# The first two key-cache loads of the sample tokens wait for the queries

## The chip, the core and the metric

The kernel runs on one core of a Trainium2 chip. The metric is the device time of one execution, in microseconds (us). A core has five engines that work side by side, each through its own queue in order: TensorE (PE; PEld is its loading of weights), VectorE (DVE), ScalarE (ACT), GpSimd (POOL) and SyncE (SP). Transfers between the chip's main memory and the on-chip memory are issued from the queues of SP, ACT and POOL and carried out by 16 DMA engines that all of them share. Matmul results go to PSUM, a small memory of eight banks.

## The reference, cut to what matters

The program is one step of one layer of a decoder, for a prompt of 512 tokens and eight sample tokens (one for each of eight sequences). One normalised input feeds a dilated sliding-window attention in three groups and an RWKV-7 time mixing; both are merged, projected, and followed by a SwiGLU network. For the sample tokens the attention reads keys and values from a cache:

```python
def dilated_window_sample(q, k_all, v_all, window, dilation, buf_len):
    T = q.shape[1]
    span = window // dilation
    idx = buf_len + jnp.arange(T)[:, None] - dilation * jnp.arange(span + 1)[None, :]
    ...
    kg = k_all[:, idx_c].astype(jnp.float32)
    vg = v_all[:, idx_c].astype(jnp.float32)
    s = jnp.einsum('bqhd,bqmhd->bhqm', q.astype(jnp.float32), kg) * HEAD_DIM ** -0.5
    p, lse = masked_softmax(s, valid[None, None])
    o = jnp.einsum('bhqm,bqmhd->bqhd', p, vg)
    return o, lse.transpose(0, 2, 1)
```

So each sample token has, for each group and head, one query, 128 cached keys and values, and its own key and value.

## The kernel before

All 520 tokens (512 + 8) go through the big products together, as two chunks of 260 columns. Each fp32 product is made of three matmuls of a shorter format: input and weights are both split in a high and a low part (`hh`/`hl` or `hu`/`lu` for the input, `whi`/`wlo` for the weights), and high x high, low x high and high x low are summed. A weight tile is loaded by SP into `raw` (512 KB), ScalarE writes `whi`, VectorE writes `wlo`.

At the start the input comes in eight tiles `xt` (260 KB each), six issued by SP and two by POOL (lines 667 to 671). Ahead of the normalisation the first products are made from the input times a weight vector only, `hu` and `lu` (lines 676 to 682), so that TensorE can begin before the sums of squares are there; `norm0` (line 703) then makes the normalised `hh` and `hl`, and half of the `hl` tiles are written by POOL (line 712).

What runs when is settled when the program is built, in two steps. A planner in the kernel (`Clocks` and `Weave`, lines 226 to 452) holds a guessed clock for each engine and a guessed cost for every instruction and transfer (a POOL load occupies POOL for 1.04 us and lands 2.7 us plus its size later). It takes the main sequence of products and the side jobs as generators, and lets that one go on whose next inputs are there by its clocks. What it writes down is then put in order once more for each engine, by a scheduler that takes what is ready; an instruction can so come to stand ahead of others that were written down before it. On the chip each queue runs in the order that came out, and an instruction whose inputs aren't there holds up all that stand behind it on its engine.

`sample_group(g)` (line 892) is such a side job, one for each of three groups. It waits until the eight query and key tiles of its group are there (line 900), lets TensorE transpose the sample columns `sga` and ScalarE copy them to `sv` (lines 903 to 910): `sv[:, 0]` are the queries, spread over 128 partitions. Then it goes through the cached keys in eight chunks of 256 KB. `cache` (line 915) loads a chunk into one of two buffers `kt` by POOL; VectorE multiplies it by the queries (line 925) and sums it into the scores `sc` (line 926). The chunk after it is always asked for one step ahead. After the softmax the values go the same way (lines 937 to 943, results in `so`), and the flag `sample` of the group is set, for which the next group's `sample_group` and the third group's first product wait. For the first group both buffers `kt` are new, so its first two loads depend on nothing that comes before them. All instructions are recorded with line 380, that of a wrapper, so the profile tells them apart by the names of their tiles.

Of the kernel before, what the change touches and what calls it, by code (L numbers as in the profile page):

```python
# [12 lines left out]
ALU = mybir.AluOpType  # L13
# [452 lines left out]
def program(tc, I, O):  # L466
    nc = tc.nc
    ck = Clocks()
    V, S, G, SY = (Unit(n, e, tc, ck) for n, e in (("DVE", nc.vector), ("ACT", nc.scalar), ("POOL", nc.gpsimd), ("SP", nc.sync)))
# [7 lines left out]
    def nm(s):  # L477
        uid[0] += 1
        return f"{s}_{uid[0]}"
# [196 lines left out]
    for k in range(KD):  # L676
        if k == 2:
            wsplit(first_w, first_raw, 4, 8)
        g = feat[:, F_MIX, k:k + 1]
# [212 lines left out]
    def sample_group(g):  # L892
# [14 lines left out]
        sv = sp.tile([128, 3, 64], FP, name=nm("sv"), tag="sv")  # L907
# [5 lines left out]
        KR = 8  # L913

        def cache(name, c):
            if c < 64:
                t = sp.tile([128, KR, 64], FP, name=nm("kt"), tag="kt", bufs=2)
                G.dma_start(out=t[:], in_=I[name][g, :, c:c + KR])
                return t
        yield from wv.take("kt")  # L920
        nxt = cache("kcache", 0)
        for c in range(0, 64, KR):
            kt, nxt = nxt, cache("kcache", c + KR)
            yield (kt,)
            V.tensor_tensor(out=kt[:], in0=kt[:], in1=_bc(sv[:, 0].unsqueeze(1), [128, KR, 64]), op=ALU.mult)
            V.tensor_reduce(out=sc[:, c:c + KR], in_=kt[:], op=ALU.add, axis=X)
            yield (sc,)
        t = sp.tile([128, 64], FP, name=nm("st"), tag="st")
# [6 lines left out]
        V.tensor_scalar(out=sc[:, 64:65], in0=sc[:, 64:65], scalar1=first[:], scalar2=None, op0=ALU.mult)  # L935
        V.tensor_reduce(out=so[:, g, 65:66], in_=sc[:], op=ALU.add, axis=X)
        nxt = cache("vcache", 0)
        for c in range(0, 64, KR):
            vt, nxt = nxt, cache("vcache", c + KR)
# [1194 lines left out]
```

## Time and profile before

| what | value |
|---|---|
| median of three runs | 1295.33 us (1294.89 to 1297.84) |
| the profiled execution's own time | 1299.81 us |
| its span | 1298.0 us |
| mean granted clock of TensorE | 0.985 |
| loads `kt<-kcache`, `kt<-vcache` | 24 each, 256 KB each |

The profile is of one execution. Its page gives the busy time of each engine and its share of the span, the DMA queues, and groups of instructions by tile; views of the trace give the instructions of one engine in order of time, who waited for whom, and tables by stretch. In a row such as "kt<-kcache" the tile that is written stands on the left and what is read on the right. In a timeline, the bracket behind a row is the idle time of that engine just ahead of it and what ended it. Busy times of TensorE are modelled ends of pipelined matmuls; the distance from start to start is the better measure of its pace.

### The profile page before, as it was taken

Reading aid. Unit: us, or ns where it says so; the run is one execution under the profiler, and the core shown is the slowest. Engines: PE = TensorE matmul, PEld = TensorE weight load, DVE = VectorE, ACT = ScalarE, POOL = GpSimd, SP = SyncE. Lnnn points to the kernel's source line nnn. Section 1 sums busy time; section 2 is a strip of 40 time slices with the busy share of each in tenths; the row PEclk is TensorE's granted clock in tenths of the full one; section 3 lists DMA queues with packets and bytes.
Section 4 is the critical chain, followed back from the end, with each engine's and each line's share of the span. In section 5 each row is a group of like instructions: output and inputs, shape, how many; then the busy total and the mean of one; then the engine's idle time right before and its main releaser. Section 6 shows DMA issues by size and latency. Waiting matters only on the chain.

```text
span 1298.0 us, 29596 instructions
## 1 busy us (share of the span) xinstructions
PE 1246.1 (96%) x11594; PEld 1178.2 (91%) x11594; DVE 933.4 (72%) x2448; ACT 648.2 (50%) x1638; POOL 176.0 (14%) x273
## 2 busy tenths in 40 slices
PE   7999999999989989999999999999999999999996
PEld 6998999989978888888888888999999999999996
DVE  6956866954769998879886765565798888873333
ACT  5244244266666655576775585323444444442220
POOL 1300100100123332122123112121000000010000
PEclk9999999999999999999998999999999999999998
DMA  6532654644245545553346355465233323343331
GB/s 218 157 95 91 209 178 146 208 137 160 73 121 152 145 143 149 153 156 104 89 126 184 101 168 169 139 218 191 92 99 98 98 98 98 98 143 90 90 103 66
DMA packets 93420, 173.76 MB, mean 134 GB/s; under 512 B 42672, under 2 KB 47824, under 8 KB 93280
## 3 DMA queue, kind: packets, MB, share of 16 engines
q1 hardware_dynamic: 60880, 102.46, 25.8%
q0 software_dynamic: 15792, 50.73, 12.9%
q10 hardware_dynamic: 16608, 18.68, 4.3%
q8 instruction: 91, 1.49, 0.5%
q14 instruction: 49, 0.40, 0.1%
HBM read 135.33 MB, written 30.07 MB: 127 GB/s over the span
## 4 chain that ended last, share of the span: by engine, by line
PE 59%; DVE 18%; issue 11%; DMA 6%; ACT 4%; POOL 2%; SPq 0%; ACTq 0%; DVEq 0%; POOLq 0%
PE mm L380 39%; PE ax L380 15%; PE ch L380 5%; DVE wlo L380 3%; DMA fb<-FD 1%; DVE X L380 1%; DVE xt L380 1%; DMA kt<-vcache 1%; DVE qk L380 1%; DVE raw L380 1%; DMA sw<-raw 1%; DVE sw L380 1%; DVE k L380 1%; DVE GH L380 1%; DVE oac L380 1%
## 5 line engine op out<-in xcount | busy, mean ns | idle before, releaser
L380 PE MATMUL mm<-hh,whi 128*128 128x260 f32 x1136 | 340.3, 300 | 0.8 <-ACT gt L380 0.8
L380 PE MATMUL mm<-hh,wlo 128*128 128x260 f32 x1136 | 326.0, 287 | 7.4 <-DVE wlo L380 7.0
L380 PE MATMUL mm<-hl,whi 128*128 128x260 f32 x1136 | 326.0, 287 | 0.0
L380 ACT CAST whi<-raw 128x1024 fp32r<-128x1024 f32 (+2 forms) x213 | 184.2, 866 | 255.8 <-PE mm L380 185.0
L380 DVE TENSOR_TENSOR wlo<-raw,whi 128x1024 fp32r<-128x1024 f32 (+2 forms) x213 | 211.5, 993 | 86.4 <-ACT whi L380 81.7
L380 PEld LDWEIGHTS mm<-hh,whi 128*128 128x128 f32 x1136 | 215.9, 190 | 13.3 <-issue 5.8
L380 PEld LDWEIGHTS mm<-hh,wlo 128*128 128x128 f32 x1136 | 216.0, 190 | 10.0 <-DVE wlo L380 9.2
L380 PEld LDWEIGHTS mm<-hl,whi 128*128 128x128 f32 x1136 | 215.9, 190 | 1.3
L380 PE MATMUL mm<-fh,whi 128*128 128x260 f32 x308 | 87.2, 283 | 0.3 <-DVE g L380 0.3
L380 PE MATMUL mm<-fh,wlo 128*128 128x260 f32 x308 | 87.1, 283 | 0.0
L380 PE MATMUL mm<-fl,whi 128*128 128x260 f32 x308 | 87.1, 283 | 0.0
L380 PE MATMUL mm<-h2l,whi 128*128 128x260 f32 x264 | 74.8, 283 | 0.0
L380 PE MATMUL mm<-h2h,wlo 128*128 128x260 f32 x264 | 74.6, 282 | 0.0
L380 PE MATMUL mm<-h2h,whi 128*128 128x260 f32 x264 | 74.6, 282 | 0.0
L380 PE MATMUL ax<-h2h,wlo 128*128 128x260 f32 x264 | 74.5, 282 | 0.0
L380 PE MATMUL ax<-h2l,whi 128*128 128x260 f32 x264 | 74.5, 282 | 0.0
L380 PE MATMUL ax<-h2h,whi 128*128 128x260 f32 x264 | 74.3, 281 | 0.0
L380 DVE TENSOR_TENSOR xt<-X,LT 128x60 f32<-128x60 f32 (+24 forms) x248 | 59.7, 241 | 3.6
L380 DVE TENSOR_TENSOR X<-X,xt 128x60 f32<-128x60 f32 (+24 forms) x248 | 56.1, 226 | 3.8
L380 PEld LDWEIGHTS mm<-fh,whi 128*128 128x128 f32 x308 | 58.1, 188 | 0.8 <-issue 0.4
L380 PEld LDWEIGHTS mm<-fh,wlo 128*128 128x128 f32 x308 | 57.9, 188 | 0.0
L380 PEld LDWEIGHTS mm<-fl,whi 128*128 128x128 f32 x308 | 57.9, 188 | 0.0
(427 smaller groups left out, 3122.0 us busy)
## 6 DMA issues: line engine op xcount, KB each, us to landing
raw<-w_in SPq DMA_DIRECT2D x77, 512.0 KB, 4.0
raw<-w_gate SPq DMA_DIRECT2D x22, 512.0 KB, 3.8
raw<-w_up SPq DMA_DIRECT2D x22, 512.0 KB, 3.8
raw<-w_down SPq DMA_DIRECT2D x16, 512.0 KB, 3.5
kt<-kcache POOLq DMA_DIRECT2D x24, 256.0 KB, 3.7
kt<-vcache POOLq DMA_DIRECT2D x24, 256.0 KB, 3.6
sw<-raw ACTq DMA_DIRECT2D x64, 65.0 KB, 3.7
GD<-gt ACTq DMA_DIRECT2D x16, 260.0 KB, 3.0
```

The source lines that it names most:

```text
L380: r = f(*a, **k)
```

## The change

In the first group (`g == 0`) and for the first two chunks of keys (`c < 2 * KR`, that is 0 and 8), POOL runs one small addition ahead of the load. It reads one column of the queries in `sv` and writes one column of the tile `kt`, which the load then fills over. As the load may only write the tile after that addition, and the addition needs `sv`, both loads come after the queries. What is computed stays the same, as the load replaces the column. The other 22 loads of keys and the 24 of values are as they were.

```diff
         def cache(name, c):
             if c < 64:
                 t = sp.tile([128, KR, 64], FP, name=nm("kt"), tag="kt", bufs=2)
+                if name == "kcache" and g == 0 and c < 2 * KR:
+
+                    G.tensor_tensor(out=t[:, 0, :1], in0=sv[:, 0, :1], in1=sv[:, 0, :1], op=ALU.add)
                 G.dma_start(out=t[:], in_=I[name][g, :, c:c + KR])
                 return t
```

`G` is POOL's wrapper, which also books the instruction on the planner's clock for POOL.

## The prediction

> **What bounds the kernel now.** I read the page first, then the waits of TensorE, and then the two stretches that the change touches: the first 20 us, where the two loads run now, and the time about 111 us, where the queries of the first group appear.
>
> ```profile
> span 1298.0 us, 29596 instructions
> ...
> PE 1246.1 (96%) x11594; PEld 1178.2 (91%) x11594; DVE 933.4 (72%) x2448; ACT 648.2 (50%) x1638; POOL 176.0 (14%) x273
> ```
>
> TensorE is busy for 1246.1 of 1298.0 us, so only 51.9 us can be won by anything that takes waits away, and a good part of these lies at the start. The next rows are the start in stretches of 1.5 us (columns: stretch, length, busy time and count on PE, PEld, DVE, ACT, POOL, then granted clock, busy share of the DMA engines, GB/s) and two rows of the DMA issues (size, and median us to landing).
>
> ```profile
> 3.00:4.50 1.50, 0.00 (x0) 0.00 (x0) 0.05 (x1) 0.00 (x0) 1.10 (x3) 1.00 0.99 316
> ...
> 9.00:10.50 1.50, 0.92 (x4) 0.62 (x4) 1.09 (x3) 0.73 (x1) 0.00 (x0) 1.00 1.01 370
> ...
> 16.50:18.00 1.50, 0.91 (x8) 0.69 (x6) 1.50 (x2) 1.50 (x5) 0.00 (x0) 1.00 1.01 385
> ```
>
> ```profile
> xt<-xT SPq DMA_DIRECT2D x6, 260.0 KB, 8.1
> kt<-kcache POOLq DMA_DIRECT2D x2, 256.0 KB, 7.0
> ```
>
> The DMA engines are full from 3 us to 18 us, and the two early key loads (512 KB) are in the middle of it: issued at 3.04 us and landed after 7.0, while the input tiles xt queue for 8.1 us. ScalarE waits for those tiles (timeline; in brackets the idle time before the row and its releaser):
>
> ```profile
> 8.21 0.61 ACT L380 CAST whi<-raw 128x512 fp32r<-128x512 f32 x1
> 9.35 0.73 ACT L380 ACTIVATE hu<-xt,feat 128x520 fp32r<-128x520 f32 x1 [0.53 <-DMA xt<-xT]
> 11.02 0.73 ACT L380 ACTIVATE hu<-xt,feat 128x520 fp32r<-128x520 f32 x1 [0.94 <-DMA xt<-xT]
> ```
>
> And TensorE waits behind it:
>
> ```profile
> 7.33 0.58 PE L380 MATMUL mm<-hu,whi 128*128 128x260 f32 x1 [7.33 <-ACT whi L380]
> ...
> 10.13 0.59 PE L380 MATMUL mm<-hu,whi 128*128 128x260 f32 x1 [0.58 <-ACT hu L380]
> ...
> 13.63 0.42 PE L380 MATMUL mm<-hu,whi 128*128 128x260 f32 x1
> 13.85 0.43 PE L380 MATMUL mm<-lu,whi 128*128 128x260 f32 x1
> 14.12 0.29 PE L380 MATMUL mm<-hu,wlo 128*128 128x260 f32 x1
> 14.24 0.28 PE L380 MATMUL mm<-hu,whi 128*128 128x260 f32 x1
> ...
> 18.04 0.39 PE L380 MATMUL mm<-hu,whi 128*128 128x260 f32 x1 [0.63 <-ACT raw L380]
> 39.27 0.39 PE L380 MATMUL mm<-hu,wlo 128*128 128x260 f32 x1 [0.82 <-DVE wlo L380]
> ```
>
> Its first matmul starts at 7.33 us, and from there to 110 us these are all the waits of its matmuls: 0.58, 0.63 and 0.82, together 2.03 us. That is what a better start can be worth, beside the matmuls' own pace.
>
> **The change: the start.** Taking 512 KB out of a full stretch that moves 316 to 370 GB/s frees 512/370 = 1.4 to 512/316 = 1.6 us of DMA time for the xt tiles behind it. ScalarE's two waits for xt, 0.53 and 0.94, make 1.47 us; I take both as gone (bounds 0 and 1.47: the tile of the 9.35 row would land about a microsecond sooner, and ScalarE is free for it at 8.21 + 0.61 = 8.82; the tile of the 11.02 row would land at about 9.5, when ScalarE has just ended the one before). TensorE's wait of 0.58 then shrinks by the same 0.53. The wait of 0.63 at 18.04 is the emptying of a PSUM bank that TensorE itself filled; it stays. The wait of 0.82 at 39.27 is for VectorE, whose work at the start hangs on ScalarE's and comes 1.47 sooner, while TensorE comes 0.53 sooner: VectorE gains 0.94 on it and the 0.82 go. Sum of the start: 0.53 + 0.82 = 1.35 us, with bounds of 0 and 2.03.
>
> **The change: about 111 us.** Now the other side (POOL first, then ScalarE's copies of the queries, VectorE's rows behind them, and TensorE's first use of the weights' low halves):
>
> ```profile
> 0.24 0.10 POOL L2126 MEMSET const-float32-0.0<- 128x1 f32 x1 [0.24 <-issue]
> ...
> 3.04 1.06 POOL L380 DMA_DIRECT2D kt<-kcache  x2
> 31.63 1.77 POOL L380 TENSOR_TENSOR hl<-hn,hh 128x520 fp32r<-128x520 f32 x1 [27.53 <-ACT hh L380]
> ...
> 54.49 3.62 POOL L380 TENSOR_TENSOR hl<-hn,hh 128x520 fp32r<-128x520 f32 x1 [3.44 <-ACT hh L380]
> ...
> 114.40 1.14 POOL L380 DMA_DIRECT2D kt<-kcache  x2 [41.93 <-DVE sc L380]
> ```
>
> ```profile
> 110.05 0.95 ACT L380 COPY sv<-ax 32x192 f32<-32x192 f32 x3
> ```
>
> ```profile
> 112.23 1.28 DVE L380 TENSOR_TENSOR kt<-kt,sv 128x512 f32<-128x512 f32 x2
> 113.43 1.27 DVE L380 TENSOR_REDUCE sc<-kt 128x8 f32<-128x512 f32 x2
> 114.76 1.22 DVE L380 TENSOR_TENSOR wlo<-raw,whi 128x1024 fp32r<-128x1024 f32 x1
> ```
>
> ```profile
> 118.20 0.29 PE L380 MATMUL mm<-hh,wlo 128*128 128x260 f32 x1
> ```
>
> The loads are written after the queries in the program, yet they head POOL's queue: its order is drawn up when the program is built, by what is ready. With the new instruction they are not ready before sv. Left at 3.04 us, they would hold up the hl rows at 31.63, on which the queries themselves depend, and the program could not end; so they go behind the last row before 114.40. Behind them in POOL's queue stands only the third load, which waits for VectorE's sc anyway: POOL sits idle 41.93 us there, and nobody else is delayed.
>
> sv is whole at 110.05 + 0.95 = 111.0. The new instruction writes one column of 128 partitions. No row shows it; its bounds are 0.10 (the memset of one column) and 3.62 (the slowest hl, 520 columns beside a busy VectorE). I take 0.3, nearest to the memset, with a little for two inputs. Then each load is issued and lands:
>
> ```profile
> L380 POOL DMA_DIRECT2D kt<-kcache x3: 536/541/543, 114.4 to 120.0; - x3
> ...
> DMA to landing us min/median/max: 3.3/3.5/4.9
> ```
>
> That row is of the next three loads of the same tile. The first lands at 111.0 + 0.3 + 3.5 = 114.8 (bounds 114.4 and 119.5), the second 0.3 + 0.54 later, at 115.6. Before, VectorE took them at 112.23: the samples' path is 2.6 us late. Its later links hang on each other, so it ends 2.6 us later too:
>
> ```profile
> 168.17 0.28 DVE L380 SCALAR_TENSOR_TENSOR so<-sv,sc,so 128x64 f32<-128x64 f32 x1
> ```
>
> ```profile
> L380 ACT COPY sv<-ax x4: 307/308/310, 205.1 to 209.2; 32x192 f32<-32x192 f32 x4
> ```
>
> The next group's queries come at 205.1, so the end may slip from 168.4 to 171.0 and nothing waits. What is displaced is VectorE's work, 1.28 + 1.27 = 2.55 us, and this has room in VectorE's idle time:
>
> ```profile
> 110.00:115.00 5.00, 5.00 (x47) 4.67 (x47) 4.25 (x8) 2.66 (x7) 0.54 (x2) 1.00 0.00 0
> ```
>
> ```profile
> 110.00:120.00 10.00, 10.00 (x86) 8.58 (x85) 8.47 (x24) 3.39 (x9) 1.08 (x2) 1.00 0.41 120
> 120.00:130.00 10.00, 10.00 (x81) 9.47 (x80) 8.11 (x21) 5.38 (x19) 1.61 (x3) 1.00 0.27 87
> 130.00:140.00 10.00, 10.00 (x97) 9.69 (x97) 7.57 (x14) 2.67 (x5) 1.07 (x2) 1.00 0.70 218
> ```
>
> VectorE is idle for 1.53 + 1.89 + 2.43 = 5.8 us from 110 to 140, twice what is displaced. The DMA engines stand still from 110 to 115 (share 0.00), so the two loads find them free. I cost this side at nothing, on the condition that VectorE's order, which is drawn up anew as well, puts the wlo row (114.76) ahead of the multiplications that now wait. If not, see the second rival.
>
> The Trainium skill speaks against this place: SBUF — State Buffer, "SBUF: two separate sides", says that a load issued from GpSimd can be starved while VectorE runs certain copies, because GpSimd cannot write its descriptors, and tells of about 3.1 us against 0.62. By it I estimate 2.5 us more on each of the two landings, 117.3 in place of 114.8. The rows of the next three loads, 536 to 543 ns to issue and 4.9 us to land at most beside a busy VectorE, show nothing of this size.
>
> **Sum.** 1.35 us off the profiled span, 1298.0 to 1296.65; with the 1.81 us around it (that execution took 1299.81) 1298.5. The runs shown have a median of 1295.33; the same step gives 1294.0.
>
> **The rivals.** *Hidden anyway:* the xt tiles land no sooner (the other loads take up the freed share), or TensorE's own pace at the start holds. For it: TensorE runs from 10.13 to 17 us almost without a wait. Against it: 0.58 and 0.82 have releasers behind the tiles. Time: 1295.3.
>
> *VectorE stands still (slower):* its queue keeps the multiplications where they are, at 112.23. VectorE then waits 114.8 - 112.2 = 2.6 us, and the second pair is done at about 117.5; wlo ends near 118.7, against its use at 118.20. It decides from the point where VectorE is over 118.20 - (114.76 + 1.22) = 2.2 us late. The price is 2.6 us there, and, as the samples' chunks stay 2.6 behind in a stretch where VectorE is busy for 9.35 of 10 us,
>
> ```profile
> 150.00:160.00 10.00, 10.00 (x87) 10.00 (x86) 9.35 (x17) 3.08 (x6) 2.09 (x4) 1.00 0.75 215
> ```
>
> a second 2.6 at most: 5.2 in all, less the 1.35 of the start: 1295.33 + 3.85 = 1299.2. Against it: until 140 us VectorE has those 5.8 us, and the order follows what is ready.
>
> *TensorE's pace steps up sooner:* matmuls start 0.22 us apart at 13.63 and 0.12 apart at 14.12 (the clock column says 1.00 throughout, so the pace is read from the starts). If the missing wait of 0.58 lets the step come as early as 10.13, some 17 matmuls (10.13 to 13.85 at 0.22) each save 0.10, 1.7 us; the low halves of the input come at VectorE's pace, so I count half, 0.85: 1293.1. The Trainium skill, TensorE: Matmul & The Clock Gate, "What's actually happening", has a window of some 3.4 us of steady work ahead of the full clock, and says that the window runs freely; by this the step would come either one whole window sooner or not at all.
>
> *A luckier order (faster):* everything after 111 us on VectorE is put in order again, and TensorE's waits for wlo change.
>
> ```profile
> PE mm L380 <- DVE wlo L380: 7.9, 7, 2.7
> ```
>
> Without the 0.82 at the start 7.1 us are left in six waits. If half of it goes, 3.5 us: 1290.5. No row says which way.
>
> **How the numbers follow.** Forecast 0.50; hidden 0.13; VectorE stands still 0.15; earlier step 0.08; luckier order 0.14. The range leaves about 0.1 out on each side: 1290.0 to 1299.5. A change of 0.3% is 3.9 us, about the least that a measurement of this kernel can tell from none: faster than 1291.4 is the luckier order and a tail of the others, 0.19; slower than 1299.2 about half of the standstill and unlucky orders, 0.13; the rest, 0.68, between. Forecast alone: 1293.3 to 1295.3.
>
> **What would show it.** Right: the kt loads issued after 111 us with a short POOL row each ahead of them; no wait of ScalarE for xt near 9 and 11 us; TensorE's waits near 10 and 39 us gone; wlo ahead of the first kt row in VectorE's queue. Wrong: xt landing as late as before; VectorE idle for over 2 us ahead of its first kt row, with TensorE waiting for wlo about 118 us; or waits of TensorE after 200 us that differ by more than the start gained.

## The result and the profile after

The changed kernel takes 1315.4 us (median of four runs, 1312.37 to 1328.0) against 1296.59 us for the kernel before, run beside it. The ratio is 1.0151, with a 95% interval from 1.0106 to 1.0196: slower by 1.5%, some 19 us, and outside the predicted range of 1290.0 to 1299.5.

The page of the changed kernel: span, busy times, and TensorE's busy share and granted clock in 40 slices of 32.8 us. Its own time was 1314.69 us, its mean granted clock 0.977 (0.985 before).

```profile
span 1312.9 us, 29600 instructions
...
PE 1254.1 (96%) x11594; PEld 1185.2 (90%) x11594; DVE 924.5 (70%) x2448; ACT 649.1 (49%) x1638; POOL 177.1 (13%) x275
...
PE   7999999999988888999998999999999999999996
...
PEclk9999999999979789998999999999999999999998
```

The same two rows of the kernel before (slices of 32.5 us):

```profile
PE   7999999999989989999999999999999999999996
...
PEclk9999999999999999999998999999999999999998
```

TensorE's idle time has grown from 51.9 to 1312.9 - 1254.1 = 58.8 us, by 6.9; the other 8.0 us are busy time, for the same 11594 matmuls. The twelfth to the sixteenth slice (361 to 525 us) all stand at 8 tenths, and the clock row has holes there that the kernel before doesn't have. All that the change itself touches lies ahead of 170 us. So the start and the place at 111 us come first, then the stretch behind.

**The start.** Stretches of 1.5 us, columns as in the prediction; the DMA issues; ScalarE's rows for `xt`; all waits of TensorE's matmuls from the start to 45 us:

```profile
9.00:10.50 1.50, 1.25 (x6) 0.95 (x6) 1.50 (x3) 1.50 (x4) 0.00 (x0) 1.00 1.06 404
16.50:18.00 1.50, 1.50 (x15) 1.48 (x14) 1.48 (x4) 1.03 (x3) 0.00 (x0) 1.00 0.07 25
```

```profile
xt<-xT SPq DMA_DIRECT2D x6, 260.0 KB, 6.6
```

```profile
7.92 0.73 ACT L380 ACTIVATE hu<-xt,feat 128x520 fp32r<-128x520 f32 x1 [0.60 <-DMA xt<-xT]
8.56 0.60 ACT L380 CAST whi<-raw 128x512 fp32r<-128x512 f32 x1
9.07 1.34 ACT L380 ACTIVATE hu<-xt,feat 128x520 fp32r<-128x520 f32 x2
```

```profile
7.38 0.58 PE L380 MATMUL mm<-hu,whi 128*128 128x260 f32 x1 [7.38 <-ACT whi L380]
9.85 0.59 PE L380 MATMUL mm<-hu,whi 128*128 128x260 f32 x1 [0.24 <-ACT hu L380]
37.93 0.39 PE L380 MATMUL mm<-hu,wlo 128*128 128x260 f32 x1 [0.89 <-DVE wlo L380]
```

The transfers are all but through by 16.5 us (share 0.07, where it was 1.01), `xt` lands after 6.6 us in place of 8.1, and ScalarE's waits of 0.53 and 0.94 are gone; a shorter one ahead of them has grown, from 0.30 to the 0.60 of the row at 7.92. The row at 37.93 stood at 39.27: 1.34 us sooner.

**At 111 us.** POOL, then VectorE:

```profile
30.27 1.77 POOL L380 TENSOR_TENSOR hl<-hn,hh 128x520 fp32r<-128x520 f32 x1 [27.23 <-ACT hh L380]
...
109.75 0.33 POOL L380 TENSOR_TENSOR kt<-sv 128x1 f32<-128x1 f32 x2 [38.28 <-ACT sv L380]
110.23 1.12 POOL L380 DMA_DIRECT2D kt<-kcache  x2 [0.15 <-POOL kt L380]
```

```profile
113.60 0.69 DVE L380 TENSOR_TENSOR kt<-kt,sv 128x512 f32<-128x512 f32 x1 [2.23 <-DMA kt<-kcache]
114.33 0.69 DVE L380 TENSOR_REDUCE sc<-kt 128x8 f32<-128x512 f32 x1
114.93 1.22 DVE L380 TENSOR_TENSOR wlo<-raw,whi 128x1024 fp32r<-128x1024 f32 x1
116.06 0.69 DVE L380 TENSOR_TENSOR kt<-kt,sv 128x512 f32<-128x512 f32 x1
```

The two additions take 0.33 us together, the loads follow at 110.23, and VectorE stands idle for 2.23 us until the first has landed. Its order is a new one: only one pair stays ahead of `wlo`, the second went behind it, so `wlo` ends at 116.15 (before, 115.98). TensorE, in stretches of 20 us:

```profile
100.00:120.00 20.00, 19.44 (x147) 16.41 (x146) 13.09 (x44) 9.31 (x28) 2.52 (x6) 1.00 0.41 118
120.00:140.00 20.00, 19.51 (x165) 17.96 (x166) 15.63 (x33) 7.92 (x24) 2.68 (x5) 1.00 0.51 164
```

It is idle for 0.56 + 0.49 = 1.05 us, where the kernel before had 20.00 of 20.00 in both. The 0.56 are a wait for VectorE's `stat` at 118.08 us. The start's gain is mostly given back here. This is a matter of one microsecond, and the loss is 15.

**Where the 15 us go.** Counting TensorE's matmuls along both traces by their starts, the changed kernel is 1.3 us ahead at the 500th (74.9 us in the kernel before), 3.2 ahead at the 2500th (320.9), 0.5 ahead at the 3300th (417.5), 13.5 behind at the 3400th (430.3), 12.0 behind at the 4000th (496.6) and 15.1 behind at the 8000th (855.6); at the 11000th it is still 15.2. Most of it is lost between 355 and 500 us, 200 us after the last load that the change moves, and the largest part of that in one place, between the 3300th and the 3400th matmul. The stretch from 355 to 500 us in the kernel before, and then in the changed one:

```profile
355.00:500.00 145.00, 129.25 (x1221) 119.10 (x1220) 126.31 (x372) 87.38 (x216) 45.49 (x63) 0.98 0.51 138
```

```profile
355.00:500.00 145.00, 123.37 (x1062) 113.05 (x1061) 108.05 (x345) 73.44 (x178) 40.85 (x55) 0.86 0.45 121
```

159 matmuls fewer in the same time, at the 145/1221 = 0.119 us that one took before 18.9 us of work; and the clock is 0.86 in place of 0.98. Two jobs run side by side there: RWKV pairs, and the merge of the attention groups, in which VectorE multiplies outputs `oo` by weights that POOL loads into `fb` from a table `FD`. VectorE's idle time that ended with one of these loads (us, times), before and after:

```profile
DMA fb<-FD: 13.3, 5
```

```profile
DMA fb<-FD: 30.0, 9
```

VectorE stands in front of `fb` for 30.0 us instead of 13.3. The tiles `oo` and `fb` take turns in the same two buffers as `kt`, so the loads for one multiplication aren't issued before the one ahead is done (POOL's row at 410.66 below waits 6.10 us for it). The dearest place, followed from engine to engine (POOL issues, VectorE waits, ScalarE waits for VectorE, TensorE for ScalarE):

```profile
410.66 0.56 POOL L380 DMA_DIRECT2D oo<-OTD  x1 [6.10 <-DVE oac L380]
411.21 1.23 POOL L380 DMA_DIRECT2D fb<-FD  x2
```

```profile
411.55 1.21 DVE L380 TENSOR_TENSOR_SCAN tw<-smask,tw 128x512 f32<-128x512 f32 x1
418.95 0.69 DVE L380 TENSOR_TENSOR oo<-oo,fb 128x512 f32<-128x512 f32 x1 [6.19 <-DMA fb<-FD]
...
421.03 0.75 DVE L380 SCALAR_TENSOR_TENSOR v<-pb,mu,v 128x511 f32<-128x511 f32 x1
...
425.98 0.75 DVE L380 SCALAR_TENSOR_TENSOR BK<-ta,feat,tw 128x512 f32<-128x512 f32 x1
```

```profile
421.87 0.38 ACT L380 COPY pb<-mm 128x260 f32<-128x260 f32 x1 [3.94 <-DVE v L380]
...
426.76 0.62 ACT L380 COPY BK<-BK 64x512 f32<-64x512 f32 x1 [3.84 <-DVE BK L380]
...
428.20 1.06 ACT L380 CAST whi<-raw 128x1024 fp32r<-128x1024 f32 x1
```

```profile
422.68 0.39 PE L380 MATMUL mm<-hh,whi 128*128 128x260 f32 x1 [1.86 <-ACT k L380]
422.90 0.28 PE L380 MATMUL mm<-hl,whi 128*128 128x260 f32 x1
429.31 0.59 PE L380 MATMUL mm<-hh,whi 128*128 128x260 f32 x1 [6.12 <-ACT whi L380]
```

Behind `oo` in VectorE's queue stand `v` and `BK`, for which ScalarE waits 3.94 and 3.84 us; behind ScalarE's copy of `BK` stands the cast of the next weights, for which TensorE waits 6.12. Then comes what doubles the price:

```profile
425.00:430.00 5.00, 0.69 (x2) 0.50 (x2) 4.97 (x21) 2.47 (x5) 0.00 (x0) 0.50 0.21 34
430.00:435.00 5.00, 3.63 (x18) 2.88 (x18) 4.36 (x15) 1.23 (x3) 1.23 (x2) 0.50 0.50 125
435.00:440.00 5.00, 5.00 (x24) 4.78 (x24) 4.69 (x12) 0.00 (x0) 0.09 (x1) 0.50 0.18 39
440.00:445.00 5.00, 5.00 (x49) 4.60 (x50) 2.50 (x4) 1.01 (x3) 2.22 (x2) 0.94 0.43 156
```

The granted clock is 0.50 from 425 to 440 us: with TensorE busy throughout, 24 matmuls in 5 us against 49 in the next 5. This is where busy time grows with the matmul count unchanged.

So most of the loss stands at a place that the changed code does not touch. The theory: **the two instructions did it through the planner.** They are booked on its clocks, its later choices come out otherwise, and another order of the whole rest is written down. In the built programs TensorE's queue has 9006 rows (equal neighbours are one row); 1763 rows differ between the two, the first of them at the third of the sixteen products `ax<-tw,lwh`, which start between 272.9 and 309.7 us. In the traces the two orders part there, at 278.7 us of the kernel before, and are the same again after 822 us. The rival: the wait itself, or the moved loads, cost the time, and the order only goes with them.

### The profile page after: what moved, and what is told of

Same layout as the page of the kernel before. It is cut to its first block, busy times and chain, and to the rows that moved or that the text cites. A ratio compares the mean times of both kernels' runs of the same rounds, so it can differ in the third digit from the quotient of the medians.

```text
span 1312.9 us, 29600 instructions
## 1 busy us (share of the span) xinstructions
PE 1254.1 (96%) x11594; PEld 1185.2 (90%) x11594; DVE 924.5 (70%) x2448; ACT 649.1 (49%) x1638; POOL 177.1 (13%) x275
## 4 chain that ended last, share of the span: by engine, by line
PE 61%; issue 15%; DVE 11%; DMA 7%; POOL 3%; ACT 3%; DVEq 0%; SPq 0%; POOLq 0%; ACTq 0%
PE mm L380 41%; PE ax L380 15%; PE ch L380 5%; DMA fb<-FD 3%; DVE wlo L380 1%; POOL kt L380 1%; DMA kt<-vcache 1%; DVE xt L380 1%; DVE X L380 1%; DVE GH L380 1%; DVE AR L380 1%; DMA br<-GTD 1%; DVE rst L380 1%; DMA tmp<-OAD 1%; POOL fb L380 1%
## 5 line engine op out<-in xcount | busy, mean ns | idle before, releaser
L380 PEld LDWEIGHTS mm<-hh,whi 128*128 128x128 f32 x1136 | 218.9, 193 | 20.1 <-ACT whi L380 6.3
L380 PEld LDWEIGHTS mm<-hl,whi 128*128 128x128 f32 x1136 | 218.8, 193 | 1.2
L380 PE MATMUL mm<-h2l,whi 128*128 128x260 f32 x264 | 74.9, 284 | 0.0
L380 DVE TENSOR_TENSOR xt<-X,LT 128x60 f32<-128x60 f32 (+22 forms) x248 | 56.8, 229 | 2.6
L380 DVE TENSOR_TENSOR X<-X,xt 128x60 f32<-128x60 f32 (+22 forms) x248 | 56.4, 228 | 3.1
```

The costliest lines, as they stand in the source:

```text
L380: r = f(*a, **k)
```

## The experiments

**The wait without the booking, and the booking without the wait.** In `wait_only` the instruction goes to the engine directly, past the wrapper that books it:

```diff
-                    G.tensor_tensor(out=t[:, 0, :1], in0=sv[:, 0, :1], in1=sv[:, 0, :1], op=ALU.add)
+                    nc.gpsimd.tensor_tensor(out=t[:, 0, :1], in0=sv[:, 0, :1], in1=sv[:, 0, :1], op=ALU.add)
```

> The small POOL addition and its wait stay, but the planner is not told of it, so that it books the two loads at the start as before and hands down the order of before. If the redrawn order costs the 1.5% (theory), the ratio to before is 0.999, within 0.997 to 1.001: about 1.3 us gained at the start, at most that lost again near 111 us. If the wait itself on the chip costs it (rival), the ratio is near 1.015.

In `booking_only` there is no instruction at all, and the planner is told of one:

```diff
-                    G.tensor_tensor(out=t[:, 0, :1], in0=sv[:, 0, :1], in1=sv[:, 0, :1], op=ALU.add)
+                    ck.run("POOL", [t[:, 0, :1]], [sv[:, 0, :1], sv[:, 0, :1]], 0.25 + 1 / 480)
```

> The reverse: the planner books the small addition, but it is not emitted, so that the loads run at 3 us as before and all engines but POOL and a stretch of VectorE have the order of the changed kernel. Theory (order): ratio 1.016, that is the changed kernel's 1.015 without the 1.3 us won at the start. Rival (wait on the chip): ratio 1.000.

Measured: `wait_only` 1295.92 us, ratio 1.0018 (0.9993 to 1.0042); `booking_only` 1313.77 us, ratio 1.0140 (1.0102 to 1.0178). The loss goes with the booking and not with the wait (`wait_only` came out a little above the range that I had written down, 0.997 to 1.001; its interval reaches into it). TensorE's matmuls follow in the traces as this says: in `wait_only` in the order of before, in `booking_only` in that of the changed kernel, one for one. In the trace of `booking_only`, whose first key loads run at the start as they did before, VectorE's waits for `fb` are again

```profile
DMA fb<-FD: 29.6, 9
```

and 13.3 in that of `wait_only`. The rival falls. Which part of the booking it is can be read from the built programs without a run: booking POOL's time alone leaves all five queues as they were, row for row; telling the planner only that the tile is ready later gives TensorE's, ScalarE's and SP's queues of the changed kernel, row for row.

**A wait for something earlier.** `wait_for_input` holds the two loads back only until the last `hl` tile is written, about 57 us, and doesn't book it:

```diff
-                    G.tensor_tensor(out=t[:, 0, :1], in0=sv[:, 0, :1], in1=sv[:, 0, :1], op=ALU.add)
+                    nc.gpsimd.tensor_tensor(out=t[:, 0, :1], in0=hl[:, 7, :1].bitcast(FP), in1=hl[:, 7, :1].bitcast(FP), op=ALU.add)
```

> As the first of these, but the small addition reads a column of the last low half hl of the normalised input (ready near 58 us in the trace before) in place of the queries, so that the loads leave the full stretch at the start and have landed long before 111 us. Theory: ratio 0.999, and, if the wait for the queries gives back the start's gain near 111 us, 1.0 to 1.4 us faster than the first of these. Rival: if any wait of these loads is dear, near 1.015.

Measured: 1295.37 us, ratio 1.0013 (0.9983 to 1.0044). It frees the start without the late landing at 111 us, and shows no gain either. TensorE's order is that of before here too.

**The change on the first load alone.** Booked as the program does it, `first_load_only` has one addition. As POOL takes its queue in order, the second load waits too:

```diff
-                if name == "kcache" and g == 0 and c < 2 * KR:
+                if name == "kcache" and g == 0 and c < KR:
```

> The change for the first of the two loads alone: one POOL instruction instead of two, booked as the program does it. POOL takes its queue in order, so the second load still waits behind the first for the queries, and the chip does nearly what the changed kernel does at 110 us; but the planner redraws almost nothing: TensorE's order differs from that of before in 9 rows of 9006 (in the changed kernel in 1763). Theory A (the handed-down order carries the loss, the wait itself is harmless): within 0.3% of the kernel before, 1291 to 1299 us, with the first half of hl on POOL 1.4 us earlier than before. Rival (waiting loads ahead of a busy VectorE carry the loss, and the order only goes with it): 0.8 to 1.5% slower, as the changed kernel.

Measured: 1299.1 us, ratio 1.0016 (0.9993 to 1.0039). In its trace the first `hl` row on POOL is early, at 29.99 us, and the addition is there:

```profile
L380 POOL DMA_DIRECT2D kt<-kcache x5: 536/536/575, 109.6 to 121.3; - x5
...
L380 POOL TENSOR_TENSOR kt<-sv x1: 188/188/188, 109.5 to 109.5; 128x1 f32<-128x1 f32 x1
```

It does on the chip what the changed kernel does at 110 us, with an order that is nearly that of before, and the 1.5% are gone. What decides is whether the planner is told that both loads wait, or only the first.

**Other orders, with no instruction changed.** If a booking alone can cost 1.4%, is the changed kernel's order an unlucky draw, or is the order of before a lucky one? `other_booking` and `other_booking_2` are the kernel before with another planner price for the hand-over between engines:

```diff
-L_SEM = 0.2
+L_SEM = 0.21
```

> Neither wait nor booking of the change: the kernel before, with the planner's guess for the hand-over between engines raised from 0.20 to 0.21 us, which redraws the order as widely as the change does (TensorE: 1905 rows of difference against 1763). Theory (the order after 111 us is a lottery of about a per cent): a ratio off 1 by 0.3% or more, in either direction, between 0.99 and 1.03. Rival (order does not matter, the wait does): 1.000, within 0.997 to 1.003.

```diff
-L_SEM = 0.2
+L_SEM = 0.19
```

> The kernel before, with 0.19 us instead of 0.20 booked by the planner for the hand-over between engines: no instruction added or moved by the edit, only the order redrawn (1560 rows of TensorE's differ). It is a second draw beside other_booking (0.21 us, 1.1% slower). Narrow form of the theory (the changed kernel's order is an unlucky one, others lie on both sides): 1285 to 1300 us. Wide form (nearly every other order loses about 1%): 1302 to 1315 us.

`smaller_booking` is the changed kernel with a lower price for its two additions:

```diff
-                    G.tensor_tensor(out=t[:, 0, :1], in0=sv[:, 0, :1], in1=sv[:, 0, :1], op=ALU.add)
+                    ck.run("POOL", [t[:, 0, :1]], [sv[:, 0, :1], sv[:, 0, :1]], 0.1 + 1 / 480)
+                    nc.gpsimd.tensor_tensor(out=t[:, 0, :1], in0=sv[:, 0, :1], in1=sv[:, 0, :1], op=ALU.add)
```

> The changed kernel's two POOL instructions, with 0.10 us booked for each instead of 0.25: the same work, a third order (1854 rows of TensorE's 9006 differ from the changed kernel's, 1647 from before's). Theory A in its narrow form (it is this one order of the changed kernel that is bad): a new order is as likely better as worse, 1288 to 1302 us. In its wide form (the order of before is a good one among many, and any other loses about 1%): 1302 to 1316 us. Rival (the wait itself costs): 1308 to 1318 us, as the changed kernel.

Measured: 1307.36 us, ratio 1.0106 (1.0068 to 1.0143); 1328.22 us, 1.0236 (1.0204 to 1.0268); 1312.72 us, 1.0126 (1.0087 to 1.0164). All three lose, `other_booking_2` more than either form of the theory had allowed (1315 us at most). Among the orders tried, that of before is the good one, and the changed kernel's an ordinary one.

**Is it the loads of `fb`?** First by price: the planner is told that each load of `fb` takes 4 us more, in the kernel before (`dear_fb_before`) and in the changed one (`dear_fb_after`):

```diff
-                t = self.ck.run(self.name, outs, ins, (2.7 if pool else 1.6) + kb / 360, 1.04 if pool else 0.45, 0.8)
+                far = 4.0 if outs[0].name.startswith("fb") else 0.0
+                t = self.ck.run(self.name, outs, ins, (2.7 if pool else 1.6) + far + kb / 360, 1.04 if pool else 0.45, 0.8)
```

> The kernel before, with 4 us more booked by the planner for each load of the merge's weights (fb); the instructions are the same, their order is a new one. Theory A (the time is lost where the planner believes fb to be there and VectorE finds it missing): VectorE's waits for fb fall from 13.3 us to under 8, and the time is the same or better, 1286 to 1297 us. Theory B: any change of a booking deals a new order, and the time lies anywhere between 1288 and 1316 us, whatever the waits for fb are.

> The changed kernel, with 4 us more booked for each load of the merge's weights (fb). Theory A: VectorE's waits for fb fall from 30.0 us to under 10, and most of the loss of 1.5% with them: 1290 to 1300 us. Theory B: a new order with a time of its own, anywhere between 1288 and 1316 us; the waits for fb may fall without the time falling.

Measured: 1306.35 us, ratio 1.0085 (1.0059 to 1.0112), and 1313.57 us, ratio 1.0120 (1.0076 to 1.0163). Theory A misses in both: VectorE's waits for `fb` do not fall, they are 21.2 us (13.3 before) and 30.5 (30.0). A dearer booking does not keep VectorE from coming to its multiplications too early; the edit only dealt two more orders.

Then without the 24 loads, all bookings kept (`no_fb_before`, `no_fb_after`). The kernel then leaves out the weighting of the attention outputs: each multiplication takes `oo` twice. The one of the first group, not shown, is replaced in the same way:

```diff
-                    G.dma_start(out=fb[H[h2]], in_=FD[:, h, g].unsqueeze(0).to_broadcast([64, 4, 128]))
+                    ck.run("POOL", [fb[H[h2]]], [FD[:, h, g].unsqueeze(0).to_broadcast([64, 4, 128])], 2.7 + fb[H[h2]].nbytes() / 1e3 / 360, 1.04, 0.8)
...
-                    V.tensor_tensor(out=ov, in0=ov, in1=fb[:], op=ALU.mult)
+                    ck.run("DVE", [ov], [ov, fb[:]], 0.07 + 512 / 960)
+                    nc.vector.tensor_tensor(out=ov, in0=ov, in1=ov, op=ALU.mult)
```

> The kernel before without the loads of the merge's weights (fb): the planner books the ten-odd loads and the multiplications that use them as it did, but the loads aren't issued, and each multiplication takes the oo tile twice instead of oo and fb, so the attention output is not weighted. Its partner is no_fb_after, which leaves the same out of the changed kernel. Before, VectorE waited 13.3 us for fb in all. Theory A (the new order loses its time in VectorE's waits for fb, at whose back stand the instructions that TensorE needs): both kernels lose these waits, so this one runs 0 to 8 us under the kernel before, 1286 to 1294 us. Theory B (the loss is spread over many waits of the new order, fb only one among them): the same here, 1286 to 1294; the two theories part in the partner.

> The changed kernel without the loads of the merge's weights, the bookings kept, as in no_fb_before (the multiplications take oo twice, so the attention output is not weighted). Theory A: the 30.0 us that VectorE waited for fb are gone, and with them nearly all of the loss: within 0.4% of no_fb_before, 1288 to 1298 us. Theory B: what remains of the new order's waits still costs: 0.8 to 1.4% over no_fb_before, 1298 to 1312 us, and the stretch from 355 to 500 us of the kernel before is passed 9 us or more later.

Measured, against the kernel before: `no_fb_before` 1290.35 us, ratio 0.9950 (0.9924 to 0.9976), and `no_fb_after` 1298.05 us, ratio 1.0011 (0.9984 to 1.0037). Between the two lie 1298.05/1290.35 = 1.0060: more than theory A allowed (0.4%) and less than theory B (0.8%). Without the loads the order costs 0.6% instead of 1.5%. The stretch from 355 to 500 us, first without the loads in the order of before, then in the changed one:

```profile
355.00:500.00 145.00, 132.67 (x1285) 122.82 (x1286) 131.52 (x396) 89.86 (x222) 32.49 (x43) 0.99 0.42 121
```

```profile
355.00:500.00 145.00, 134.28 (x1285) 124.09 (x1284) 123.44 (x389) 86.64 (x213) 32.65 (x39) 0.95 0.42 123
```

Both do 1285 matmuls, where 1221 and 1062 stood with the loads. But the dearest place is still there. From 420 to 440 us, the kernel before and the changed one:

```profile
420.00:440.00 20.00, 20.00 (x170) 18.65 (x170) 18.74 (x65) 11.27 (x29) 6.27 (x9) 1.00 0.44 120
```

```profile
420.00:440.00 20.00, 10.65 (x50) 9.06 (x50) 18.88 (x63) 4.75 (x11) 4.06 (x7) 0.59 0.33 74
```

The same without the loads, in the order of before and in the changed one:

```profile
420.00:440.00 20.00, 19.15 (x154) 18.12 (x153) 19.49 (x67) 9.72 (x26) 4.88 (x7) 1.00 0.40 120
```

```profile
420.00:440.00 20.00, 13.35 (x78) 11.67 (x77) 16.81 (x62) 4.56 (x10) 2.35 (x4) 0.74 0.34 97
```

With no load of `fb` to wait for, the changed order still does 78 matmuls where the order of before does 154, at a granted clock of 0.74. TensorE's waits there in `no_fb_after`:

```profile
425.31 0.39 PE L380 MATMUL mm<-hh,whi 128*128 128x260 f32 x1 [4.09 <-ACT sho L380]
427.06 0.59 PE L380 MATMUL ax<-ident,sg 128*16 128x128 f32 x2 [1.15 <-DVE sg L380]
429.07 1.22 PE L380 MATMUL ax<-svd,uk 48*128 48x256 f32 x2 [1.41 <-POOL svd L380]
```

ScalarE's `sho` stands behind its copy of `BK`, for which it waits 2.00 us for VectorE here (3.84 with the loads). From the 3300th to the 3400th matmul the changed order falls back against that of before by 14.0 us with the loads and by 9.2 without them. So the waits for `fb` are not the whole cause. By the medians more than half of the loss goes with the loads (18.8 us with them, 7.7 without); at the dearest place about a third does, and the rest of that place stays with the order, in which TensorE comes to these instructions of the RWKV pair before the other engines have got so far. What else parts these two comes later: they are 2.0 us apart at the 4000th matmul and 12.9 at the 8000th. It is not settled, since leaving out the loads also moved rows (some 25 in TensorE's queue of the one, about a hundred in that of the other), and the two profiled executions lie 13.2 us apart where the medians differ by 7.7.

How far each kernel is behind the one before, in us, at the start of some matmuls of TensorE (one execution each). After 834 us of the kernel before all of them run the same matmuls in the same order; ahead of that a redrawn order has other matmuls under the same number, so that a lag there is good to a few us only:

| matmul (time in the kernel before) | 500 (74.9) | 2500 (320.9) | 3300 (417.5) | 3400 (430.3) | 4000 (496.6) | 5000 (576.3) | 8000 (855.6) | 11000 (1216.4) |
|---|---|---|---|---|---|---|---|---|
| changed | -1.3 | -3.2 | -0.5 | 13.5 | 12.0 | 18.1 | 15.1 | 15.2 |
| booking_only | -0.2 | -1.6 | 0.3 | 13.0 | 10.7 | 18.8 | 14.6 | 14.6 |
| wait_only | -1.8 | -2.1 | -1.4 | -1.4 | -1.8 | -1.7 | -2.4 | -2.4 |
| wait_for_input | -0.9 | -2.4 | -2.9 | -1.3 | -1.7 | -0.4 | -1.6 | -1.6 |
| first_load_only | -1.6 | 1.1 | 2.3 | 3.5 | 3.0 | 4.2 | 5.4 | 5.5 |
| other_booking | 0.2 | -2.2 | 2.9 | 3.8 | 4.5 | 9.3 | 7.8 | 7.8 |
| other_booking_2 | -0.2 | -2.2 | 1.1 | 6.1 | 5.4 | 3.8 | 23.0 | 23.4 |
| smaller_booking | -1.5 | -1.7 | 4.5 | 5.2 | 10.7 | 9.7 | 7.3 | 7.4 |
| dear_fb_before | 0.8 | 1.1 | 5.9 | 5.2 | 9.3 | 8.9 | 10.4 | 10.4 |
| dear_fb_after | -1.2 | -3.5 | -0.4 | 8.4 | 7.1 | 9.4 | 15.9 | 15.9 |
| no_fb_before | -0.2 | 1.7 | 1.4 | 2.3 | -3.8 | -3.5 | -13.9 | -13.9 |
| no_fb_after | -0.9 | 2.1 | -0.4 | 9.7 | -1.8 | 0.1 | -1.0 | -0.9 |

A single execution can stand several us from its kernel's median (the one of `first_load_only` took 1305.2, the median is 1299.1), so the small differences say little. The large ones agree: at the 2500th matmul (320.9 us) every redrawn order is within 4 us of the kernel before, and at the 4000th (496.6 us) it is 4 to 12 us behind; `other_booking_2` loses most, 17.6 us, between the 4000th and the 8000th. Its own waits for `fb` are 18.7 us, those of `other_booking` 14.1, hardly above the 13.3 of before. So the waits for `fb` carry much of the loss in the changed order, and not in each of them.

## Why the prediction was wrong

*The start, 1.35 us.* It came: TensorE's row at 39.27 moved by 1.34 us and the `hl` row on POOL by 31.63 - 30.27 = 1.36. That the sum fits so well is luck, as its two terms were not the right ones. The wait of 0.58 shrank to 0.24, not by the full 0.53; the wait for `wlo` stayed (0.82, then 0.89), and the wait of 0.63 that I left standing went. Three waits of 2.03 us in all became 1.13, which is 0.90 of the 1.34 us; the rest I have not placed. I had also left out ScalarE's first short wait, which grew by 0.30. TensorE's faster pace came at 13.95 instead of 14.12 us, so the rival that it steps up earlier was not it.

*The added instruction and the loads.* 0.33 us for both, where I took 0.3 for each; loads at 110.23, where I had about 111.3; first multiplication at 113.60, where I had 114.8. The rule that I quoted from the Trainium skill, SBUF — State Buffer, "SBUF: two separate sides", would have put it at 117.3. The load issued at 110.23 had landed 3.4 us later, so the trace doesn't show the starved load here; but VectorE stood idle for 2.23 of these 3.4 us, which is hardly a test of it.

*VectorE at 111 us, at nothing.* Half right. VectorE did stand still, 2.23 us (I priced the standstill at 2.6), but the condition under which it is dear, `wlo` late by over 2.2 us, did not hold: 0.17 late. TensorE lost 1.05 us from 100 to 140 us. With the start's gain that is about nothing, as `wait_only`, `wait_for_input` and `first_load_only` show (1.0018, 1.0013, 1.0016): what the change does on the chip is worth less than 0.5% either way by their intervals (0.9983 to 1.0044), and a gain is not shown. Had the order stayed, the time would have been near that of before, and the forecast gain of 1.35 us too small to see.

*The step that failed.* It is the one that I called "a luckier order (faster)": "everything after 111 us on VectorE is put in order again, and TensorE's waits for wlo change", worth 3.5 us at most, with "No row says which way". It was wrong in three ways. The place: it isn't VectorE's `wlo` waits after 111 us that decide; TensorE's own queue comes out otherwise too, from 278.7 us on, and the loss lies in the merge behind 355 us. The size: not 3.5 but 15 us in the trace. And the sign: I gave the fast side a rival of its own at 0.14 and the slow side a part of the 0.13. A row that I had quoted leans one way: TensorE was busy for 96% of the span. The 51.9 us of idle time bound all that another order can win by taking waits away, while no row bounds what it can lose. Six other orders were run (the changed one, `other_booking`, `other_booking_2`, `smaller_booking` and the two with dear `fb`), and all six lose, 0.85 to 2.4%.

I wrote that waits of TensorE after 200 us that differ by more than the start gained would prove the prediction wrong. That is what came: from 360 to 500 us the changed kernel's list of TensorE's waits begins with

```profile
PE mm L380 <- ACT whi L380: 6.1, 1, 6.1
PE ax L380 <- POOL svd L380: 5.3, 2, 3.9
PE ch L380 <- DVE AR L380: 3.6, 1, 3.6
```

where the longest before were 2.7 us for `wlo` and 3.2 for `sd`.

What stays open: why the order of before meets so few of these waits (its prices may have been chosen because their order ran well, which no run here shows), what part of the loss behind 420 us is not the waits for `fb`, what costs `other_booking_2` its time after the 4000th matmul, and whether an order better than that of before can be had. None of the kernels run here beats it with the full computation.

## What to carry to other kernels

Where a planner inside the kernel books every instruction, an added instruction is two changes: what it does on its engine, and the order that the planner then deals to everything behind it. Test them apart, the instruction unbooked and the booking without the instruction, before anything is concluded from the sum. And where the bound engine is already busy for 96%, as here, a redrawn order is not a coin that may fall either way: the six of this kernel lost 0.85 to 2.4%, and none won. What it costs in another kernel no run here shows.

## What the runs showed of the hardware that I had not expected

A wait on TensorE costs more than its length. After waits of 1.86 and 6.12 us the granted clock stood at 0.50 for 15 us, though TensorE ran 3.63 of the 5 us from 430 to 435. From 433.06 us on it ran without a break, first small products (16 of `ax<-AR,BK`), and after 435.92 us full ones; the clock came back at about 440.4 us, 7.4 us after the small ones began and 4.5 us after the full ones. The Trainium skill, TensorE: Matmul & The Clock Gate, "What's actually happening", has two states, half and full clock, and a window of some 3.4 us of sustained work to leave the lower one. The two states agree with the trace, and so does the 4.5 us for a window that runs freely; by that figure I estimate that one whole window before it, from some 433.6 to 437.0 us, was busy throughout and did not bring the clock back, with small products in most of it. It also says that such a ramp is under 1% of a typical span. 15 us at half clock cost 7.5 us, 0.6% of the span, which agrees; with the waits that set it off the place holds 120 matmuls fewer from 420 to 440 us (50 against 170), at 0.119 us each some 14 us or 1.1%, most of which is lost for good.

The two loads of one `fb` tile, issued from 411.21 us on, kept VectorE until 418.95, 7.7 us later. One of the two was the slowest of all 24 in the changed kernel, where such a load lands after 4.6 us in the median and 7.0 at most:

```profile
DMA to landing us min/median/max: 2.9/4.6/7.0
```

They were issued right behind the load of `oo` (410.66 us) in the same queue, and a weight load of 512 KB issued by SP at 411.98 us took 6.6 us beside them (4.1 in the median of `raw<-w_in`), with the DMA engines 95% busy from 412 to 416 us. Which of this makes the difference was not tried.
